# Attention scores over half the partitions: the second score matmul on the two halves of the TensorE array in turn

## The chip, the cores and the metric

The kernel runs on one core of one Trainium2 chip. The metric is the device time of one execution in microseconds (us); lower is better. The kernel before took 701.67 us, the median of three runs between 701.51 and 701.72.

## What is computed

The reference is one decoder layer in float32 for 512 tokens of width 1024: a pooling mixer and a sparse attention side by side, merged by gates, then a gated MLP with a short convolution. The change touches the attention scores. Cut to those:

```python
q  = partial_rope(rms_norm(q, q_norm_g), positions)        # 8 heads of 64, 2 groups of 4 heads
ks = partial_rope(rms_norm(k_sel, k_norm_g[1]), positions) # "selected" keys, one per group
kw = partial_rope(rms_norm(k_win, k_norm_g[2]), positions) # "window" keys, one per group
s  = jnp.einsum('bqgrd,bkgd->bgrqk', qc, kwc) * scale      # and the same with the selected keys
p  = masked_softmax(s, m_win, -1)
o  = jnp.einsum('bgrqk,bkgd->bqgrd', p, vwc)
```

With 512 tokens every block is selected and the window holds every earlier token, so both branches are causal attention, each with its own keys and values.

## The kernel before, in words

**Products in two parts.** Each operand is kept as a high and a low part, both in the type fp32r, and a product is the sum of matmuls over those parts. For the scores a head has only 64 dimensions, so the kernel stacks the parts of q on the 128 partitions: `qk_transpose` (L706 to L721) turns `qs` (per token the high 64 values beside the low 64) into `QT[g, t]`, with the high part of q on partitions 0 to 63 and the low part on 64 to 127, for four heads of group g and the 128 tokens of tile t. The keys are stored twice over: `KT[0, t]` holds the high part of k on both halves, `KT[1, t]` the low part on both halves. One matmul over all 128 partitions with `KT[0]` then gives high times high plus low times high; a second with `KT[1]` gives high times low plus low times low.

**Scores.** `scores(h, i)` (L940) computes head h for the 128 queries of tile i against the n = i + 1 key tiles up to it: for each key tile j two matmuls (s = 0 and 1) with 128x128 weights from `QT` and 256 moving columns (128 window keys and 128 selected keys) from `KT`, all in one unit that is not broken up on TensorE. Key tiles 0 and 1 fall in one PSUM bank and 2 and 3 in another. Units with n above 2 use the tag `sc` (one buffer), the others the tag `tr`. One head has four units with n from 1 to 4, 20 matmuls; eight heads have 32 units and 160 matmuls. After it come the softmax on VectorE and ScalarE (tiles `pp`, `asm`), the transposes of the probabilities (`transposes`, L975), the product with the values (`av`, L987) and `av_out` (L1011). The loop at L1034 goes through the heads; while head h is transposed and multiplied with the values, the scores of head h + 1 are computed, for i = 3, 2, 1, 0 in steps 0, 3, 6 and 10 of the head. So the units with the `QT` of group 0 end in head 2, and the last of group 1 in head 6.

**Two streams on TensorE.** The attention belongs to a stream "m". Beside it runs a stream "f" (L746 to L827): 22 "features", each 24 matmuls of 128x128 weights by 512 columns (`feature`, L733), whose results go through a pooling chain (`pool_in`, L759, pages `u`, `ps`, `pm`, `pmh`, `pml`), a small product (`mix`, L785, pages `yph` and `ypl`, kept until the last `pool_out`), or a gate (`gate`, L777, page `th`, written to DRAM and freed). In order: two features for the compressed keys, `pool_in(0)`, then three times `pool_in`, `gate`, `mix`, then a last `gate` and `mix`, then the rest of the gates with four `pool_out`.

**The planner.** No order is written out. Every call is recorded (`Plan.note`, L157) with a price (`Plan.price`, L197; for a matmul by its moving columns alone), and `Plan.run` (L226) makes an order for all engines: on TensorE each stream keeps its own order and the planner picks between the two heads of the streams; on the other engines it takes the ready operation that is due first. `Plan.emit` (L374) tries 12 orders. On the chip, each engine then runs its list strictly in that order.

**Pages.** Most tiles are "pages" of 128 partitions by 512 words, drawn from one pool of 54 (`PAGES`, L51). A page is held from its first writer to its last reader. The rule at L288 lets an operation of stream f take a page only while more than `RESERVE` = 3 pages (L61) are free, so stream f can fill the pool up to 51 and no further; stream m may use all 54.

While the attention runs, stream m and the inputs hold 16 pages of the normalised input (`xh`, `xl`, needed by every feature), 4 of values (`vv`), 8 of `QT`, 8 of `KT`, 4 zero-padded probability tiles (`PZ`, L969) and 1 or 2 of compressed scores (`cs`); later 2 pages of attention output (`oh`, `ol`) are added after each second head.

Of the kernel before, what the change touches and what calls it, by code (L numbers as in the profile page):

```python
# [9 lines left out]
F32R = mybir.dt.float32r  # L10
# [5 lines left out]
P = 128  # L16
# [380 lines left out]
def hybrid_layer(ctx: ExitStack, tc: tile.TileContext, xT, pos, par, cst, poolw, w1, wa, wb, wf,  # L397
# [3 lines left out]
    PE, ACT, DVE, POOL, SP = pl.engines  # L401
# [5 lines left out]
    def f32(ap):  # L407
        return ap.bitcast(F32)

    def page(name, shape=(P, T), dt=F32):  # L410
        return pl.tile(sb, shape, dt, name, "pg", PAGES)
# [6 lines left out]
    def keep(name, shape, dt=F32, bufs=1):  # L418
        return pl.tile(sb, shape, dt, name, "t_" + name, bufs)

    def bank(tag, shape=(P, T)):
        return pl.tile(ps, shape, F32, tag, tag, {"mm": 2, "tr": 3, "av": 1, "sc": 1}[tag], psum=True)

    def split(dst_hi, dst_lo, src, scale=None):
        if scale is None:
            ACT.activation(dst_hi, src, AF.Copy)
            DVE.tensor_sub(dst_lo, src, f32(dst_hi))
        else:
            ACT.activation(dst_hi, src, AF.Copy, scale=scale)
            DVE.scalar_tensor_tensor(dst_lo, src, scale, f32(dst_hi), op0=ALU.mult, op1=ALU.subtract)  # L430
# [62 lines left out]
    pt = bank("mm")  # L493
# [153 lines left out]
    for t in range(NT):  # L647
        pt = bank("mm")
# [21 lines left out]
    def rope_on(x, tmp, idx, n):  # L670
        np_ = x.shape[0]
        ct = rope[:np_, 0, idx].rearrange("p a b -> p (a b)")
        for o, i in ((0, 1), (1, 0)):
            DVE.tensor_mul(tmp[:, :, o * 8:(o + 1) * 8], x[:, :, i * 8:(i + 1) * 8],
                           rope[:np_, 1, idx, o][:, None, :].to_broadcast([np_, n, 8]))
        DVE.tensor_mul(x[:, :, 0:16], x[:, :, 0:16], ct[:, None, :].to_broadcast([np_, n, 16]))
        DVE.tensor_add(x[:, :, 0:16], x[:, :, 0:16], tmp)
# [3 lines left out]
    def rope_split(t):  # L681
        x, y = qp[t], kp[t]
        DVE.tensor_mul(x[:, :, 0:16], x[:, :, 0:16], gq[:, None, :].to_broadcast([P, 8, 16]))
        y4 = y.rearrange("p (b g) d -> p b g d", b=2)
        DVE.tensor_mul(y4, y4, gkv[:, 1:3][:, :, None, :].to_broadcast([P, 2, 2, DH]))
        tmp = page("rt", (P, 12, 16))
        rope_on(x, tmp[:, 0:8], t, 8)
        rope_on(y, tmp[:, 8:12], t, 4)
        qs = [page("qs", (P, 4, 2, DH), F32R) for _ in range(2)]
        ks = [page("ks", (P, 4, 2, DH), F32R) for _ in range(2)]  # L690
        for g in range(2):
            split(qs[g][:, :, 0], qs[g][:, :, 1], x[:, 4 * g:4 * g + 4])
        kx = y[:, :, None, :].to_broadcast([P, 4, 2, DH])
        split(ks[0], ks[1], kx)
        qsp.append(qs)
        ksp.append(ks)

    for t in range(NT):
        x, y = qp[t], kp[t]
# [1 line left out]
        DVE.tensor_mul(y, pskt[:, t // 2, t % 2].rearrange("p (h d) -> p h d", d=DH),  # L701
                       rs_t[:, t, 8:12][:, :, None].to_broadcast([P, 4, DH]))
    pl.span = [pl.last().i, 0]
    QT, KT = {}, {}

    def qk_transpose(t):  # L706
        for g in range(2):
            pt = bank("tr", (P, 4, P))
            with pl.unit():
                for i in range(4):  # L710
                    PE.transpose(pt[:, i], f32(qsp[t][g][:, i].rearrange("p a d -> p (a d)")), ident)
            QT[g, t] = page("qt", (P, 4, P), F32R)
            ACT.activation(QT[g, t], pt, AF.Copy)
        for s in range(2):
            pt = bank("tr", (P, 2, 2, P))
            with pl.unit():
                for g in range(2):
                    for b in range(2):
                        PE.transpose(pt[:, g, b], f32(ksp[t][s][:, 2 * b + g].rearrange("p a d -> p (a d)")), ident)
            KT[s, t] = page("kt", (P, 2, 2, P), F32R)  # L720
            ACT.activation(KT[s, t], pt, AF.Copy)  # L721

    rope_split(0)
    rope_split(1)
    turned = []
    for t in range(NT):
        qk_transpose(t)
        turned.append(pl.last())
        if t + 2 < NT:
            with pl.behind(turned[t]):  # L730
                rope_split(t + 2)

    def feature(i, hi, lo):  # L733
        wh, wl = weights(flat(wf[i]), 1024)
        pt = bank("mm")
        mm3(pt, wh, wl, hi, lo, 0, KD)
        return pt
# [8 lines left out]
    with pl.on("f"):  # L746
        for i in range(2):
            pt = feature(i, xh, xl)
# [81 lines left out]
    for i in range(2):  # L830
# [4 lines left out]
        pt = bank("tr")  # L835
# [20 lines left out]
    x = keep("kcx", (64, 1, DH))  # L856
# [83 lines left out]
    def scores(h, i):  # L940
        g, hh = divmod(h, 4)
        n = i + 1
        pt = bank("sc", (P, 4, 2, P)) if n > 2 else bank("tr", (P, 2, 2, P))
        with pl.unit():
            for j in range(n):
                for s in range(2):
                    PE.matmul(pt[:, j], QT[g, i][:, hh], KT[s, j][:, g], start=(s == 0 and j % 2 == 0),
                              stop=(s == 1), skip_group_check=True)
        sm = keep("asm", (P, 4, 2), bufs=4)
        if n > 2:  # L950
            pp = [pl.tile(sb, (P, T), F32, "pp", "pp", 10)[:, :n * P].rearrange("p (j k) -> p j k", k=P) for _ in range(2)]
        else:
            x = pl.tile(sb, (P, T), F32, "pp", "pp", 10).rearrange("p (b j k) -> p b j k", b=2, k=P)
            pp = [x[:, b, :n] for b in range(2)]
        for b in range(2):
            DVE.tensor_tensor_reduce(out=pp[b], in0=pt[:, 0:n, b], in1=mask[:, NT - n:NT], scale=1.0,
                                     scalar=3.0e38, op0=ALU.add, op1=ALU.min, accum_out=sm[:, 0, b:b + 1])
        for b in range(2):
            ACT.activation(pp[b], pp[b], AF.Exp, bias=sm[:, 0, b:b + 1], scale=-1.0,
                           accum_out=sm[:, 1, b:b + 1])  # L960
        DVE.reciprocal(sm[:, 2], sm[:, 1])
        DVE.tensor_mul(sm[:, 3], sm[:, 2], gates[:, i, 3 * h + 1:3 * h + 3])
        for b in range(2):
            DVE.tensor_scalar_mul(pp[b], pp[b], sm[:, 3, b:b + 1])
            Pt[h, b, i] = pp[b]
# [56 lines left out]

    compress_kt()
    scores(0, 0)
    cmp_scores(0)
    cmp_scores(1)
    scores(0, 1)
    cmp_softmax(0)
    scores(0, 2)
    scores(0, 3)  # L1030
    extra = {(0, 2 * i + 2): (lambda i=i: cmp_transpose(0, i)) for i in range(NT)}
# [20 lines left out]
    def any_bank():  # L1052
        turn[0] += 1
        return bank(("mm", "tr", "tr", "mm", "tr", "av")[turn[0] % 6])

    mh, ml, nots = [], [], []
    for c in range(4):
        wh, wl = weights(wno[c].rearrange("p a k n -> p (a k n)"), 1024, "v")
        for f in (2 * c, 2 * c + 1):
            o = (f % 2) * 512  # L1060
            pt = any_bank()
# [21 lines left out]
    for f in (0, 4, 1, 5, 2, 6, 3, 7):  # L1083
# [4 lines left out]
        pt = any_bank()  # L1088
# [228 lines left out]
    for f in range(8):  # L1317
        wh, wl = weights(flat(wdz[f]), 768, "v")
        pt = any_bank()
# [6 lines left out]
        for h in range(2):  # L1326
            s = slice(h * H2, (h + 1) * H2)
            pt = any_bank() if h else pt
            for k in range(16, KF):
                c = slice((k - 16) * P, (k - 15) * P)  # L1330
                with pl.unit():
                    for j, (w, q) in enumerate(((wh, yh), (wh, yl), (wl, yh))):
                        PE.matmul(back(pt[:, :H2]), w[:, c], back(q[k][:, s]), start=k == 16 and j == 0,
                                  stop=k == KF - 1 and j == 2)
# [97 lines left out]
```

## Time and profile before

| | us |
|---|---|
| median of three runs | 701.67 |
| the profiled execution | 701.34 |
| its span | 699.6 |
| TensorE matmuls busy | 693.0 |
| TensorE weight loads busy | 612.9 |
| VectorE busy | 479.1 |
| ScalarE busy | 434.4 |
| GpSimd busy | 102.9 |

The profile is of one execution. The span runs from the first to the last instruction; the execution's own time is 1.7 us more. PE is the matrix part of TensorE and PEld its weight loads; a matmul's end in the trace is modelled and matmuls overlap in the pipeline, so the time from one start to the next is what a matmul costs when the engine is full, not its duration. DVE is VectorE, ACT ScalarE, POOL GpSimd, SP the engine that only issues DMAs. Nearly every instruction has line 393, the place where the planner's order is sent out, so groups are told apart by their tiles: `sc<-kt,qt` is a score matmul with a result in the tag `sc`. A shape as 64*128 behind MATMUL or LDWEIGHTS gives the active rows and columns of the array.

### The profile page before, as it was taken

How to read it: one execution, taken by the hardware profiler on the slowest of the kernel's cores; microseconds unless marked ns; L12 is line 12 of the kernel's file. 1: busy time of each engine (PE TensorE's matmuls, PEld its weight loads, DVE VectorE, ACT ScalarE, POOL GpSimd, SP SyncE). 2: the span in 40 equal slices, each digit the busy share in tenths (PEclk: the TensorE clock that was granted, in tenths of full speed). 3: DMA queues.
4: the chain of work that ended last, by engine and by line, in shares of the span. 5: the costliest groups of instructions: out<-in, count | busy, mean ns of one | idle time of the engine just before them, and what ended most of it. 6: DMA issues, size and time to landing. Idle time of an engine off the chain costs nothing.

```text
span 699.6 us, 11376 instructions
## 1 busy us (share of the span) xinstructions
PE 693.0 (99%) x4160; PEld 612.9 (88%) x4160; DVE 479.1 (68%) x1025; ACT 434.4 (62%) x794; POOL 102.9 (15%) x127
## 2 busy tenths in 40 slices
PE   9999999999999999999999999999999999999998
PEld 8898888888888888888888898999999999999987
DVE  6868488777866653685559876777777776766542
ACT  7667378766776663443358866776777766674320
POOL 0011300010011010000012222321312212220000
PEclk9999999999999999999999999999999999999999
DMA  8576352555565657854468878897988877865131
GB/s 296 171 181 203 85 121 77 135 138 120 135 166 144 157 125 212 297 164 138 151 145 207 186 177 172 205 202 181 216 191 196 198 167 178 179 144 123 45 125 64
DMA packets 45704, 114.01 MB, mean 163 GB/s; under 512 B 5328, under 2 KB 6096, under 8 KB 45648
## 3 DMA queue, kind: packets, MB, share of 16 engines
q1 hardware_dynamic: 29664, 76.57, 33.8%
q0 software_dynamic: 15840, 36.71, 29.2%
q8 instruction: 33, 0.54, 0.3%
q14 instruction: 23, 0.19, 0.1%
q10 hardware_dynamic: 144, 0.01, 0.0%
HBM read 70.27 MB, written 6.29 MB: 109 GB/s over the span
## 4 chain that ended last, share of the span: by engine, by line
PE 96%; DMA 2%; issue 1%; DVE 1%; ACT 0%; POOL 0%; SPq 0%; POOLq 0%; DVEq 0%; ACTq 0%
PE mm L393 41%; PE tr L393 30%; PE sc L393 13%; PE av L393 11%; DMA sl<-r 1%; DMA xr<-xT 1%; POOL sl L393 0%; DVE th L393 0%; DVE kc L393 0%; ACT kt L393 0%; SPq L393 0%; DVE ks L393 0%; ACT qs L393 0%; ACT ks L393 0%; ACT xh L393 0%
## 5 line engine op out<-in xcount | busy, mean ns | idle before, releaser
L393 ACT ACTIVATE whi<-wraw 128x1024 fp32r<-128x1024 f32 (+2 forms) x97 | 98.0, 1011 | 70.0 <-issue 27.2
L393 DVE TENSOR_TENSOR wlo<-wraw,whi 128x1024 fp32r<-128x1024 f32 (+1 forms) x66 | 76.3, 1158 | 15.1 <-ACT whi L393 13.3
L393 POOL DMA_DIRECT2D wlo<-wraw x30 | 26.0, 868 | 329.9 <-ACT wlo L393 257.7
L393 PE MATMUL mm<-xh,whi 128*128 128x512 f32 x176 | 73.5, 417 | 0.9 <-DVE kc L393 0.6
L393 PE MATMUL mm<-xh,wlo 128*128 128x512 f32 x176 | 69.0, 392 | 0.0
L393 PE MATMUL mm<-xl,whi 128*128 128x512 f32 x176 | 69.0, 392 | 0.0
L393 PE MATMUL mm<-tl,sh 128*128 128x256 f32 x190 | 53.5, 282 | 0.0
L393 PE MATMUL mm<-th,sl 128*128 128x256 f32 x174 | 49.1, 282 | 0.0
L393 PE MATMUL mm<-th,sh 128*128 128x256 f32 x174 | 49.0, 281 | 0.0
L393 POOL DMA_DIRECT2D sl<-r x36 | 31.0, 862 | 89.8 <-ACT sl L393 53.4
L393 ACT ACTIVATE pp<-pp,asm 128x384 f32<-128x384 f32 (+3 forms) x64 | 35.4, 556 | 11.6 <-DVE asm L393 11.4
L393 ACT ACTIVATE wlo<-wraw 128x1024 fp32r<-128x1024 f32 x30 | 31.7, 1056 | 15.3 <-PE mm L393 6.6
L393 DVE SCALAR_TENSOR_TENSOR ft<-fg,pr,ft 128x511 f32<-128x511 f32 (+1 forms) x44 | 33.0, 749 | 12.0 <-ACT ft L393 11.3
L393 PE MATMUL sc<-yh,whi 128*128 128x512 f32 x104 | 40.5, 389 | 0.0
L393 PE MATMUL sc<-yl,whi 128*128 128x512 f32 x104 | 40.5, 389 | 0.0
L393 PE MATMUL sc<-yh,wlo 128*128 128x512 f32 x104 | 40.5, 389 | 0.0
L393 PEld LDWEIGHTS mm<-xh,wlo 128*128 128x128 f32 x176 | 33.0, 188 | 7.5
L393 PEld LDWEIGHTS mm<-xh,whi 128*128 128x128 f32 x176 | 33.2, 189 | 6.2 <-DVE th L393 1.1
L393 PEld LDWEIGHTS mm<-xl,whi 128*128 128x128 f32 x176 | 33.3, 189 | 3.6
L393 PEld LDWEIGHTS mm<-tl,sh 128*128 128x128 f32 x190 | 35.7, 188 | 0.4
L393 PEld LDWEIGHTS mm<-th,sh 128*128 128x128 f32 x174 | 32.8, 188 | 1.0
L393 PEld LDWEIGHTS mm<-th,sl 128*128 128x128 f32 x174 | 32.7, 188 | 0.0
(397 smaller groups left out, 2101.2 us busy)
## 6 DMA issues: line engine op xcount, KB each, us to landing
wlo<-wraw POOLq DMA_DIRECT2D x30, 512.0 KB, 4.6
wraw<-wup SPq DMA_DIRECT2D x26, 512.0 KB, 4.0
wraw<-wf SPq DMA_DIRECT2D x22, 512.0 KB, 3.6
r<-wup SPq DMA_DIRECT2D x36, 256.0 KB, 5.4
sl<-r POOLq DMA_DIRECT2D x36, 256.0 KB, 5.2
wraw<-wdn SPq DMA_DIRECT2D x16, 512.0 KB, 4.3
sl<-s POOLq DMA_DIRECT2D x18, 256.0 KB, 5.3
sl<-wraw POOLq DMA_DIRECT2D x18, 256.0 KB, 4.6
```

The lines of the kernel that those rows point to most:

```text
L393: getattr(self.real[o.eng], method)(*a, **kw)
```

## The change

The second score matmul leaves out low times low: it multiplies only the high part of q with the low part of k, over the 64 partitions that hold that part. For key tiles 0 and 1 (first PSUM bank) it uses partitions 0 to 63, for key tiles 2 and 3 (second bank) partitions 64 to 127, and with more than two key tiles the order is 0, 2, 1, 3, so that halves and banks alternate. The first matmuls of all key tiles now come first and the second ones after them. The number of matmuls, their moving columns and their 128 weight columns stay as they were.

For this the high part of q must lie on both halves. Group 1 now has it on the upper half from the start (the split writes high to place g and low to place 1 - g), and a new page `Q2[t]` per token tile gets, by two DMAs on GpSimd's queue, the high part of group 0 on the upper half and that of group 1 on the lower half. These are 8 DMAs of 64 partitions by 512 words (128 KB each) and 4 pages, held from the transposes to the last scores of head 7. `PAGES`, `RESERVE` and the planner's prices are unchanged.

```diff
         for g in range(2):
-            split(qs[g][:, :, 0], qs[g][:, :, 1], x[:, 4 * g:4 * g + 4])
+            split(qs[g][:, :, g], qs[g][:, :, 1 - g], x[:, 4 * g:4 * g + 4])
...
-    QT, KT = {}, {}
+    QT, KT, Q2 = {}, {}, {}
...
             QT[g, t] = page("qt", (P, 4, P), F32R)
             ACT.activation(QT[g, t], pt, AF.Copy)
+        Q2[t] = page("q2", (P, 4, P), F32R)
+        POOL.dma_start(Q2[t][64:128], QT[0, t][0:64])
+        POOL.dma_start(Q2[t][0:64], QT[1, t][64:128])
...
             for j in range(n):
-                for s in range(2):
-                    PE.matmul(pt[:, j], QT[g, i][:, hh], KT[s, j][:, g], start=(s == 0 and j % 2 == 0),
-                              stop=(s == 1), skip_group_check=True)
+                PE.matmul(pt[:, j], QT[g, i][:, hh], KT[0, j][:, g], start=(j % 2 == 0), stop=False,
+                          skip_group_check=True)
+            for j in ((0, 2, 1, 3) if n > 2 else (0, 1)):
+                if j < n:
+                    a = j // 2
+                    r = slice(a * 64, (a + 1) * 64)
+                    PE.matmul(pt[:, j], (QT[g, i] if a == g else Q2[i])[r, hh], KT[1, j][r, g], start=False, stop=True,
+                              skip_group_check=True)
```

## The prediction

> **What bounds the kernel now.** First the page: the engines' busy time and the chain that ended last.
>
> ```profile
> span 699.6 us, 11376 instructions
> PE 693.0 (99%) x4160; PEld 612.9 (88%) x4160; DVE 479.1 (68%) x1025; ACT 434.4 (62%) x794; POOL 102.9 (15%) x127
> PE 96%; DMA 2%; issue 1%; DVE 1%; ACT 0%; POOL 0%; SPq 0%; POOLq 0%; DVEq 0%; ACTq 0%
> ```
>
> TensorE is the bound: it is busy 99% of the span and carries 96% of the chain. A microsecond added to or taken from its full stream is one of the kernel's, and a stretch in which it runs dry is lost. Next, the timeline and the tile view place the change: all 160 score matmuls lie between 92 and 252 us, and the scores of heads 3 and 7 begin (for i = 3) at 144 and 236. Window sums over the stretches between those marks say what covers what.
>
> ```profile
> L393 PE MATMUL sc<-kt,qt x112: 274/282/364, 97.6 to 240.7; 128*128 128x256 f32 x112
> L393 PE MATMUL tr<-kt,qt x48: 274/282/388, 92.1 to 251.8; 128*128 128x256 f32 x48
> 144.00 0.51 PE L393 MATMUL sc<-kt,qt 128*128 128x256 f32 x3
> 235.67 0.51 PE L393 MATMUL sc<-kt,qt 128*128 128x256 f32 x3
> 97.00:144.00 47.00, 46.83 (x273) 40.10 (x272) 39.51 (x128) 36.45 (x81) 4.31 (x5) 1.00 0.46 113
> 144.00:188.00 44.00, 43.91 (x243) 36.81 (x242) 35.09 (x108) 31.91 (x68) 4.31 (x5) 1.00 0.55 139
> 188.00:236.00 48.00, 48.00 (x269) 40.36 (x268) 29.42 (x91) 33.00 (x69) 5.17 (x6) 1.00 0.57 142
> ```
>
> The columns are length, then PE, PEld, DVE, ACT and POOL busy, the clock, and DMA. In all three stretches PE is full, DVE is not far behind in the first two, and the clock is 1.00. PE is full only because stream f fills what the attention (stream m) leaves.
>
> **The change part by part.**
>
> *Matmuls.* Their number stays 160. Eight of them in a row, and the next of another kind behind, give the cost of one:
>
> ```profile
> 214.39 1.11 PE L393 MATMUL sc<-kt,qt 128*128 128x256 f32 x8
> 215.35 0.40 PE L393 MATMUL mm<-xh,whi 128*128 128x512 f32 x1
> ```
>
> 0.96 us for 8 is 0.12 each. If two matmuls on different halves ran side by side, i = 3 would save two of its four second matmuls and i = 2 one of three; i = 0 and 1 stay in one half. Three per head, 24 in all, at most 24 x 0.12 = 2.9 us; at least nothing. No row of the trace shows such a pair, so both ends stay.
>
> A rule that promises the upper end: the Trainium skill, TensorE: Matmul & The Clock Gate, section "Part 3: Packing small matmuls", says that matmuls on different row groups run concurrently, starting some 4 ns apart. By it the term is the full 2.9 us. The same page, "LDWEIGHTS (loading the stationary operand)", holds that a load costs by its columns (128/1.2 = 107 ns) whatever its rows; if loads went one by one, a pair would cost two of them and the term would be about 0.01 us a matmul. No run so far decides.
>
> *Going to 64 rows and back.* The trace has one place where the array works on 64 rows: the two transposes of `kcsp`.
>
> ```profile
> 91.31 0.39 PE L393 MATMUL mm<-xl,whi 128*128 128x512 f32 x1
> 91.54 0.39 PE L393 MATMUL mm<-xh,wlo 128*128 128x512 f32 x1
> 91.86 0.34 PE L393 MATMUL tr<-cs,kcsp 64*128 64x64 f32 x2
> 92.12 0.51 PE L393 MATMUL tr<-kt,qt 128*128 128x256 f32 x2
> 92.47 0.39 PE L393 MATMUL mm<-xh,whi 128*128 128x512 f32 x1
> ```
> ```profile
> 91.86 0.20 PEld L393 LDWEIGHTS tr<-cs,kcsp 64*128 64x128 f32 x2 [0.35 <-issue]
> 92.12 0.30 PEld L393 LDWEIGHTS tr<-kt,qt 128*128 128x128 f32 x2
> ```
> ```profile
> L393 ACT ACTIVATE kcsp<-kcx x1: 289/289/289, 89.7 to 89.7; 64x128 fp32r<-64x128 f32 x1
> L393 DVE TENSOR_TENSOR kcsp<-kcx,kcsp x1: 275/275/275, 90.2 to 90.2; 64x128 fp32r<-64x128 f32 x1
> ```
>
> Matmuls of 512 columns start 0.23 apart, with the next weights loaded meanwhile. Here the load comes only at 91.86, 0.32 after the last start, although its data were there at 90.5, and the profile calls the wait "issue": it waited for nothing that is recorded. The way back shows the same: the load at 92.12 starts together with its matmul, not ahead of it. From 91.54 to 92.47 pass 0.93 us. One matmul of 512 (0.23) and two of 256 (0.24) leave 0.46 for two small transposes, which cost 0.05 to 0.11 each (the higher is the cost of one with twice the columns, below). So a visit to 64 rows costs 0.24 to 0.35 us beyond its matmuls. A score unit has larger weights to load in the open, some 0.05 more: 0.24 to 0.40, and I take 0.32, near the middle since this is the one row. Against it stands another shape, the 128*64 matmuls of `av`:
>
> ```profile
> 206.81 0.39 PE L393 MATMUL mm<-yph,wlo 128*128 128x512 f32 x1
> 207.03 0.28 PE L393 MATMUL av<-pz,vv 128*64 128x256 f32 x1
> 207.15 0.49 PE L393 MATMUL tr<-cs,pp 128*128 128x128 f32 x3
> ```
>
> They come 0.22 behind and are followed 0.12 later: no gap (and three transposes in 0.49 with 0.27 for the last give 0.11 each). So not every smaller shape stops the array; but that one halves columns, and the 64 rows of the change are what `kcsp` has. With 32 units, each once to 64 rows and back, the price is 32 x 0.32 = 10.2 us (7.7 to 12.8) wherever PE is full.
>
> The Trainium skill, TensorEngine Tiling, "Key Properties", says that a change of tiling mode drains the array. For 64 rows the trace agrees, 0.32 instead of 0.23; for 64 columns, also a mode of that page, it does not (0.22 and 0.12).
>
> *DMAs.* Eight more on GpSimd's queue. Nearest rows:
>
> ```profile
> L393 POOL DMA_DIRECT2D wlo<-wraw x4 | 3.5, 869 | 31.8 <-ACT wlo L393 24.7 <-PE tr L393 7.1
> sl<-r POOLq DMA_DIRECT2D x36, 256.0 KB, 5.2
> L393 ACT ACTIVATE qt<-tr x8: 581/596/601, 54.6 to 71.5; 128x512 fp32r<-128x512 f32 x8
> ```
>
> 0.87 us of issue each, 7 us of an engine that between 50 and 100 us issues four DMAs and idles; about 5 us to land. The last copy of `QT` starts at 71.5 and the first score at 92.1, so 20 us hide 8. Behind a waiting DMA on that queue stand the weights' `wlo` transfers of stream f; the order puts them where they fit. I count 0, at most 2 us if a feature's weights are late once.
>
> *Pages.* This is the part that I think decides. The pool and the reserve stay, and four pages more are held until head 6. By the code, stream m and the inputs hold 16 + 4 + 8 + 8 + 4 + 1 = 41 pages in the first stretch; f may fill up to 51, so it has 10 and would have 6. After head 3 they hold 40 (`QT` of group 0 gone, four of output added), and with `Q2` 44: f has 11 and would have 7. What f needs: 2 pages of pooling weights, 2 for a group that is pooled and waits for its product, 2 more for every product done (kept to the end of the stream), and 3 at work in a pooling chain.
>
> *Stretch 1* (97 to 144; heads 0 and 1). What f did here before, and how fast attention's other engine could go alone:
>
> ```profile
> L393 PE MATMUL mm<-xh,whi 128*128 128x512 f32 x38 | 15.8, 416 | 0.2 <-DVE th L393 0.2
> ```
>
> 38 triples of 512 columns are 38 x 3 x 0.23 = 26 us, with two products 27; so m had 20 of the 47. With 6 pages f can still send TensorE two gates' features, one product and one pooling feature, 3 x 24 x 0.23 + 0.7 = 17 us; then both `mm` banks hold results for which there is no page. PE has 20 + 17 = 37, and 12 units x 0.32 = 3.8 of stops: 41 us. DVE's 39.5 falls to some 36, so PE still bounds: the stretch ends earlier, f is 10 us behind, and **3.8 us** are lost.
>
> *Stretch 2* (144 to 188; heads 2 and 3). m on PE per head: 20 scores at 0.12, 20 transposes at 0.11, per branch two matmuls each of 512, 384, 256 and 256 columns (2.6 in all), one of 512: 7.4 us. Two heads and four transposes more are 15.2; f had 28.8. Now f holds 6, may have 9, and gets through two features and two products, 12.3. PE: 27.5. DVE's 35.1 loses four or five f operations, about 3 us, and at 95% busy needs 34. Lost: **6.5 us**.
>
> *Stretch 3* (188 to 236; heads 4 and 5). f now keeps 8 (2 weights, 4 outputs, 2 pooled) but 44 + 8 is over 51: it stands still until `QT`, `KT` and `Q2` fall free in head 6. PE has m's 16.5 (two heads, 16 small transposes). DVE of before, less f's:
>
> ```profile
> L393 DVE TENSOR_TENSOR th<-mm,rb 128x512 f32<-128x512 f32 x5 | 3.5, 692 | 2.4 <-PE mm L393 2.3
> L393 DVE SCALAR_TENSOR_TENSOR th<-th,mm 128x512 f32<-128x512 f32 x2 | 1.4, 683 | 1.1 <-PE mm L393 1.1
> ```
>
> 29.4 - 4.8 = 25, at 93% 27 us. Lost: **10.5 us**; the stops hide in it. What f left undone, 10 + 16.5 + 31.5 = 58 us (48 - 16.5 = 31.5 in this stretch), is then done on PE behind the attention at its full price.
>
> *Sum.* Four units ahead of 97 and four behind 236 add 8 x 0.32 = 2.6. 3.8 + 6.5 + 10.5 + 2.6 = 23.4 us on the profiled execution's 701.34 (span 699.6 and 1.7 around it): 724.7, and since the median is 0.3 above that execution, **725 us**. Side-by-side pairs would take off at most 1.5 where PE is full; I take nothing. If DVE worked without a gap, stretches 2 and 3 would lose 4 us less; at 80% they would lose 10 more; with 0.24 and 0.40 a visit the stops move by 2. That makes 718 to 738 for this case.
>
> **The rivals.**
>
> *Only the stops count.* The planner picks among 12 orders and could fit f into fewer pages (a pooling chain before its neighbour, more f before 97). For it: PE was full with f at its limit too. Against: the counts above leave no room for the eight pages of f in stretch 3. Then 7.7 to 12.8 less up to 2.9, with 0.32 some 7 to 10: 706 to 714, likeliest 710.
>
> *No stops, only pages.* If fp32r matmuls of 64 rows pass as those of `av` do, the 6.4 us of stops in the sum go: 716 to 724, likeliest 718.
>
> *Faster: halves side by side.* Neither stops nor pages bind, and the 24 pairs overlap wholly: 701.67 - 2.9 = 698.8. The point from which it decides: a visit must cost under 2.9/32 = 0.09 us, the third part of what the `kcsp` row shows, and f must lose nothing. By the Trainium skill, TensorE: Matmul & The Clock Gate, section "Part 3: Packing small matmuls", the pairs would give just this.
>
> *The change does nothing.* No stops, pages fit, and pairs run one behind the other: 701.5 to 702.
>
> **How the numbers follow.** Pages and stops 0.58; stops alone 0.25; pages alone 0.07; faster 0.06; nothing 0.04. The range takes most of the first three, 709 to 738, and leaves out the last two and the tails, some 0.2. A measurement of this kernel tells about 0.2% (1.4 us) from no change; so faster 0.06, same 0.04, slower 0.90.
>
> **What would show it.**
>
> ```profile
> L393 DVE TENSOR_TENSOR th<-mm,rb x16: 680/692/693, 106.1 to 285.4; 128x512 f32<-128x512 f32 x16
> ```
>
> *Stops:* score rows of shape 64*128, their weight loads idle before with "issue", and a visit 0.24 to 0.40 us longer than its matmuls; if the second matmuls follow at 0.12 without a gap, that step is wrong. If in a unit with four key tiles the second ones start in pairs closer than 0.12, side by side is right. *Pages:* PE busy below 90% between about 140 and 220 us, idle ahead of score and transpose rows with DVE or ACT as releaser, the features' rows `mm<-xh` thinned out there and pushed behind the attention, and the gates' `th` row above ending far later than 285.4. If PE stays at 99% busy there and the `mm<-xh` matmuls keep their places, the page step is wrong and 710 is the time. *DMAs:* `q2` rows landing before 85 us; if scores wait for them, that zero is wrong.

## The result, and the profile after

The changed kernel takes 732.95 us, the median of four runs between 731.2 and 735.68; the kernel before took 701.59 beside it (701.33 to 701.72). The ratio is 1.0451, with a 95% interval of 1.0434 to 1.0469: 31 us slower. The forecast was 725, with a range of 709 to 738.

The page of the changed kernel: span, engines, the busy tenths of PE and its clock in 40 slices of 18.2 us, and the chain that ended last.

```profile
span 729.4 us, 11394 instructions
PE 708.9 (97%) x4160; PEld 618.1 (85%) x4160; DVE 482.0 (66%) x1025; ACT 434.0 (59%) x794; POOL 107.4 (15%) x135
PE   9999999897789999999999999999999999999998
PEclk9999999999899999999999999999999999999999
PE 92%; DVE 4%; DMA 1%; ACT 1%; issue 1%; POOL 0%; ACTq 0%; POOLq 0%; DVEq 0%
```

PE now has a hole in the slices from 128 to 219 us, and the chain has DVE in it. No other engine became the bound of the whole; the hole sits in the attention. The scores of heads 3, 5 and 7 begin (i = 3) at 139.2, 174.8 and 203.5 instead of 144.0, 188.0 and 235.7. Window sums over the stretches between these marks, with the columns as in the prediction:

```profile
97.00:139.20 42.20, 40.59 (x230) 32.04 (x229) 31.71 (x107) 30.97 (x74) 3.46 (x4) 1.00 0.40 94
139.20:174.80 35.60, 30.33 (x170) 23.90 (x169) 30.04 (x96) 24.82 (x58) 1.72 (x2) 1.00 0.33 83
174.80:203.50 28.70, 22.87 (x131) 17.87 (x130) 21.86 (x77) 18.39 (x51) 0.00 (x0) 0.88 0.00 1
```

The attention goes faster, since it has TensorE to itself, and in the third stretch not one weight tile is loaded: DMA is 0.00 and POOL, which sends the low parts of the filler's weights, does nothing. The filler stream f stands still. Its matmuls by stretch, from the groups of PE (97 to 139.2, 139.2 to 174.8, and 203.5 to 316; the third stretch has none):

```profile
L393 PE MATMUL mm<-xh,whi 128*128 128x512 f32 x24 | 10.5, 438 | 0.0
L393 PE MATMUL mm<-xh,whi 128*128 128x512 f32 x16 | 6.2, 390 | 0.0
L393 PE MATMUL mm<-xh,whi 128*128 128x512 f32 x104 | 41.9, 403 | 0.1
```

Eight of these are one feature. Three features, two, none, and then thirteen from the scores of head 7 on. Where f stops shows at its last feature ahead of the hole: the last matmul of it, and the next DVE instruction that takes a result of f, into the new page `u`.

```profile
157.12 0.40 PE L393 MATMUL mm<-xh,wlo 128*128 128x512 f32 x1
202.66 0.67 DVE L393 TENSOR_TENSOR u<-mm,rb 128x512 f32<-128x512 f32 x1
```

Between them lie 45 us in which no matmul of a feature runs, though TensorE has idle time: finished results wait to be taken. That it is the page they wait for is tested below. The last gate shows what that costs at the end:

```profile
L393 DVE TENSOR_TENSOR th<-mm,rb x16: 680/691/692, 111.9 to 315.6; 128x512 f32<-128x512 f32 x16
```

315.6 against 285.4 is 30.2 us later, and the span grew by 29.8. What follows takes its old time: 729.4 - 315.6 = 413.8 us against 699.6 - 285.4 = 414.2.

The stops are there too. One unit with four key tiles in the timeline, first PE, then PEld (`q` is `Q2`):

```profile
101.38 0.40 PE L393 MATMUL mm<-xh,wlo 128*128 128x512 f32 x1
101.61 0.94 PE L393 MATMUL sc<-kt,qt 128*128 128x256 f32 x5
102.18 0.38 PE L393 MATMUL sc<-kt,q 64*128 64x256 f32 x1
102.40 0.28 PE L393 MATMUL sc<-kt,qt 64*128 64x256 f32 x1
102.40 0.28 PE L393 MATMUL sc<-kt,q 64*128 64x256 f32 x1
102.61 0.50 PE L393 MATMUL mm<-xh,whi 128*128 128x512 f32 x1
102.95 0.39 PE L393 MATMUL mm<-xl,whi 128*128 128x512 f32 x1
```
```profile
102.18 0.18 PEld L393 LDWEIGHTS sc<-kt,q 64*128 64x128 f32 x1
102.28 0.19 PEld L393 LDWEIGHTS sc<-kt,qt 64*128 64x128 f32 x1
102.28 0.19 PEld L393 LDWEIGHTS sc<-kt,q 64*128 64x128 f32 x1
102.61 0.19 PEld L393 LDWEIGHTS mm<-xh,whi 128*128 128x128 f32 x1
```

A merged row carries the shape of its first instruction: of the five in the row at 101.61 the fifth is already a 64-row matmul; its partner on the other half has the row at 102.18. Two things are to be seen. The second matmuls run in pairs: two start at 102.40, and their loads both at 102.28. And on the way in and out the load starts with its matmul instead of ahead of it (102.18 and 102.61 in both fences), as at `kcsp`. From the unit's start to the second matmul behind it pass 102.95 - 101.61 = 1.34 us; eight matmuls at 0.12 and one of 0.23 would be 1.19. So with two pairs gained this visit still costs 0.15.

### The profile page after: what moved, and what is told of

Its sections match the earlier page's. It is cut to its first block, busy times and chain, and to the rows that moved or that the text cites. A ratio compares the mean times of both kernels' runs of the same rounds, so it can differ in the third digit from the quotient of the medians.

```text
span 729.4 us, 11394 instructions
## 1 busy us (share of the span) xinstructions
PE 708.9 (97%) x4160; PEld 618.1 (85%) x4160; DVE 482.0 (66%) x1025; ACT 434.0 (59%) x794; POOL 107.4 (15%) x135
## 4 chain that ended last, share of the span: by engine, by line
PE 92%; DVE 4%; DMA 1%; ACT 1%; issue 1%; POOL 0%; ACTq 0%; POOLq 0%; DVEq 0%
PE mm L393 40%; PE tr L393 29%; PE sc L393 13%; PE av L393 11%; DVE pp L393 1%; DMA sl<-r 1%; DVE pt L393 1%; DVE pz L393 0%; ACT pt L393 0%; POOL sl L393 0%; DVE kc L393 0%; DVE pm L393 0%; ACT kt L393 0%; DVE u L393 0%; ACT ptc L393 0%
## 5 line engine op out<-in xcount | busy, mean ns | idle before, releaser
L393 ACT ACTIVATE pp<-pp,asm 128x128 f32<-128x128 f32 (+3 forms) x64 | 35.4, 556 | 10.0 <-DVE asm L393 9.6
```

Of the source, the lines that this page charges most:

```text
L393: getattr(self.real[o.eng], method)(*a, **kw)
```

## The experiments

Each ran beside the kernel before on the same chip. In the first four that took 701.67 us, in the last four 701.79.

| kernel | us | ratio, 95% interval |
|---|---|---|
| four pages and the transfers alone | 723.13 | 1.029 to 1.0321 |
| 64 rows, one half, no page | 713.37 | 1.0153 to 1.0196 |
| the change, no page more (packed) | 711.05 | 1.0123 to 1.0154 |
| the change, two pages more | 718.63 | 1.0235 to 1.0277 |
| four pages alone, `RESERVE` = 1 | 712.71 | 1.0137 to 1.0207 |
| before, `RESERVE` = 1 | 701.5 | 0.9986 to 1.0005 |
| the eight transfers alone | 701.62 | 0.9987 to 1.0006 |
| the change for four key tiles alone | 702.57 | 1.0002 to 1.0021 |

**Theory:** the pool's rule starves f, and 64-row visits stop TensorE; two costs that stand beside each other. **Rivals:** only the stops count; only the pages count; the transfers carry part of it.

### The pages alone

```diff
+        Q2[t] = page("q2", (P, 4, P), F32R)
+        POOL.dma_start(Q2[t][64:128], QT[1, t][64:128])
+        POOL.dma_start(Q2[t][0:64], QT[1, t][0:64])
...
-                    PE.matmul(pt[:, j], QT[g, i][:, hh], KT[s, j][:, g], start=(s == 0 and j % 2 == 0),
+                    PE.matmul(pt[:, j], (Q2[i] if s and g else QT[g, i])[:, hh], KT[s, j][:, g], start=(s == 0 and j % 2 == 0),
```

> The four pages and the eight DMAs alone: all score matmuls over 128 partitions; Q2 is a plain copy of group 1's q, taken by the second matmuls of heads 4 to 7. If the page pool starves the filler stream (my theory), the filler features stand still in heads 2 to 5 as in the changed kernel and some 20 to 24 us are lost: 721 to 726 us, PE busy about 85% between 140 and 205 us. If the stops for 64 rows are what costs (rival), this is 701.5 to 703 us.

723.13 us, 21.5 above before: pages cost what the theory says, without one 64-row score matmul. Its windows between the same marks (scores of heads 3, 5 and 7 at 136.7, 170.3 and 196.5):

```profile
97.00:136.70 39.70, 37.73 (x229) 31.91 (x228) 31.69 (x107) 30.71 (x74) 3.43 (x4) 1.00 0.42 101
136.70:170.30 33.60, 28.82 (x171) 23.81 (x170) 29.48 (x97) 24.56 (x58) 1.71 (x2) 1.00 0.33 88
170.30:196.50 26.20, 19.63 (x132) 17.00 (x131) 21.95 (x77) 18.47 (x51) 0.00 (x0) 0.93 0.00 1
```

The third stretch has the same empty DMA column. Against the changed kernel each stretch is 2.0 to 2.5 us shorter. PE's share is 86% in the second and 75% in the third, where "about 85%" was expected.

### The stops alone

```diff
-        Q2[t] = page("q2", (P, 4, P), F32R)
-        POOL.dma_start(Q2[t][64:128], QT[0, t][0:64])
-        POOL.dma_start(Q2[t][0:64], QT[1, t][64:128])
...
-            for j in ((0, 2, 1, 3) if n > 2 else (0, 1)):
+            for j in (range(4)):
                 if j < n:
-                    a = j // 2
-                    r = slice(a * 64, (a + 1) * 64)
-                    PE.matmul(pt[:, j], (QT[g, i] if a == g else Q2[i])[r, hh], KT[1, j][r, g], start=False, stop=True,
+                    r = slice(g * 64, (g + 1) * 64)
+                    PE.matmul(pt[:, j], QT[g, i][r, hh], KT[1, j][r, g], start=False, stop=True,
```

> The 64-row matmuls alone: no Q2, no page more; the second matmuls of a group all use the half on which its high part of q lies, so none run side by side. Theory: PE stays full and 32 visits to 64 rows at 0.38 to 0.42 us each add 12 to 13 us: 713 to 715 us. If the stops are hidden or the pages are all there is (rival): 701.5 to 704 us. If only the pages were in the trace and stops are 0.24 each: 709.

713.37 us: 11.7 above before, 0.37 a visit. PE stays full, so every stop is paid. Its page and, in the timeline, a unit with four key tiles (the row of eight holds four matmuls over 128 rows and four over 64):

```profile
PE 705.3 (99%) x4160; PEld 616.1 (87%) x4160; DVE 479.6 (67%) x1025; ACT 435.3 (61%) x794; POOL 102.7 (14%) x127
```
```profile
101.50 1.30 PE L393 MATMUL sc<-kt,qt 128*128 128x256 f32 x8
102.73 0.50 PE L393 MATMUL mm<-xh,whi 128*128 128x512 f32 x1
103.07 0.39 PE L393 MATMUL mm<-xl,whi 128*128 128x512 f32 x1
```

103.07 - 101.50 = 1.57, less the 1.19 worked out above: 0.38 for the visit. Against 1.34 with the two pairs, a pair saves (1.57 - 1.34) / 2 = 0.115 us, a whole matmul.

### The change without more pages

`Q2` for tiles 2 and 3 alone, and the low keys in two pages:

```diff
...
-            KT[s, t] = page("kt", (P, 2, 2, P), F32R)
-            ACT.activation(KT[s, t], pt, AF.Copy)
+            if s == 0 or t < 2:
+                KT[s, t] = page("kt", (P, 2, 2, P), F32R)
+            else:
+                KT[s, t] = KT[s, t - 2]
+            r = slice(0, P) if s == 0 else slice(t // 2 * 64, (t // 2 + 1) * 64)
+            ACT.activation(KT[s, t][r], pt[r], AF.Copy)
...
```

> The change with no page more than before: Q2 only for token tiles 2 and 3 (two pages), and the low part of the keys packed into two pages instead of four, since each tile's is read on one half only. The 64-row matmuls and their pairs are those of the change. Theory: the page loss is gone, the stops stay, and 24 pairs side by side take 24 x 0.117 = 2.8 us off the one-half kernel: 710 to 712 us, 2.8 us below the kernel with one half. If pairs gain nothing: as that kernel. If the stops had been hidden: below 704.

711.05 us, 9.4 above before and 2.3 below the kernel with one half (forecast 2.8). By the two intervals that difference could be anything from 0 to 5 us; that a pair gains is shown by the timelines, 1.57 against 1.34, and not by these medians. The stops with the pairs are 9.4 us, the pages alone 21.5; together 30.9, and the change measured 31.4. So nearly the whole loss is accounted for. That the sum meets so closely is partly luck, since the starved kernels also ran some time at half clock, the changed one longest (last section). This also makes a better form of the change, but no better kernel.

### Two pages more

The packed kernel with the low keys in four pages again.

> As the packed kernel, but the low keys in four pages: two pages more than before instead of none or four. Theory: a dose between 711 and 733 us; with f allowed 8 instead of 6 pages in heads 0 and 1 and 9 in heads 4 and 5, most of the stall goes: 713 to 722, I say 717. If pages do not matter: equal to the packed kernel within 1 us.

718.63 us: two pages cost 7.6 over the packed kernel, four cost 732.95 - 711.05 = 21.9. The cost grows faster than the pages.

### The rule

```diff
-RESERVE = 3
+RESERVE = 1
```

on the kernel with the pages alone, and as a control on the kernel before.

> The kernel with the pages alone (all matmuls over 128 partitions) with RESERVE = 1 instead of 3, so that stream f may fill the pool up to 53 and gets two of the four pages back. Theory: it is this rule that starves f, and the loss falls as with two pages fewer held, by about two thirds: 706 to 714 us against 723. Rival: the m stream or a chip resource suffers from the extra pages and transfers, and the rule is not what binds: 720 to 726.

> Control for it: the kernel before with RESERVE = 1. Theory: TensorE is full there, two pages more for f gain nothing: 700.5 to 703 us. If the limit already cost something before: below 700.

712.71 us, its runs lying between 712.13 and 717.8: by the medians half of the loss is gone (two thirds were expected), with the same pages, transfers and matmuls, by two pages that f may take. The control, 701.5, cannot be told from before. The rule costs time, and only with the four pages held.

### The transfers alone

```diff
+    q2d = [pl.tile(dr, (P, 4, P), F32R, "q2d", "q2d", 4) for _ in range(4)]
...
+        POOL.dma_start(q2d[t][64:128], QT[0, t][0:64])
+        POOL.dma_start(q2d[t][0:64], QT[1, t][64:128])
```

> The eight transfers alone: the kernel before, with the same eight DMAs of 64 partitions by 512 words on GpSimd's queue, written to DRAM, so that no page is held, and read by nothing. Theory: 0 to 1 us: 701 to 703. If the transfers carry part of the 21.5 us of the pages kernel (rival): above 705.

701.62 against 701.79: nothing. These transfers go to DRAM and nothing reads them, so the run shows the price of issuing and moving them. In the changed kernel itself the eight are issued between 55.6 and 79.4, each lands within 8.1 us, and no matmul is seen to wait for one. That rival is out.

### Only where two pairs can be had

```diff
+            for j in range(n if n < 4 else 0):
+                PE.matmul(pt[:, j], QT[g, i][:, hh], KT[1, j][:, g], start=False, stop=True, skip_group_check=True)
-            for j in ((0, 2, 1, 3) if n > 2 else (0, 1)):
+            for j in ((0, 2, 1, 3) if n > 3 else ()):
```

with `Q2` for tile 3 alone.

> The change for units with four key tiles alone (i = 3): 8 visits instead of 32, 16 pairs instead of 24, Q2 for one token tile (one page more than before). Theory: 8 x (0.38 - 2 x 0.115) = 1.2 us for the visits and 0 to 3 for the page: 703 to 706. If a visit's price grew with its matmuls so that pairs pay: below 701.

702.57 us, 0.8 above before (0.1 to 1.5 by the interval) and a little under the 703 to 706 expected: the visits are 8 x 0.15 = 1.2 by the timeline. Here the page cost nothing that shows. Even the units with the most pairs do not gain.

## Why the prediction was right, point by point

*Direction and the two causes.* Both steps held: the `kcsp` row gave the stop, the count of pages gave the stall, and each alone makes the kernel slower.

*What f gets through.* Forecast 24, 16 and 0 matmuls with `whi` of `xh` (three features, two, none); measured 24, 16 and 0. Of the small products it counted one, two and none; one, one and none came. The lengths of the stretches were forecast at 41, 34 and 27 us and came out at 42.2, 35.6 and 28.7.

*The price of a visit.* Taken as 0.32 from bounds of 0.24 and 0.40; it is 0.38, and the pairs, counted at nothing, are worth 0.115 each. With both, 32 x 0.38 - 24 x 0.115 = 9.4, which is what the packed kernel measures (8.9 with the 11.7 that the kernel with one half measures for 32 visits). That the trace's one row was read at its middle and not at the end with larger loads is a small error.

*The step that failed: "the stops hide in it".* The forecast held that where f stands still the attention is bound by DVE at 93 to 95% busy, so stops on an idle PE cost nothing, and counted 6.4 us of them. In the second stretch they cost something: from the pages kernel to the changed one it grew from 33.6 to 35.6, both at a clock of 1.00, where the packed kernel's average of 9.4 / 32 = 0.29 for 8 visits is 2.3. In the third, for which the forecast said it, the growth from 26.2 to 28.7 is not all theirs: up to the scores at 193.21 in the changed kernel and at 188.05 in the other (both rows in the last section) it is 18.4 against 17.75 us at full clock, 0.7 for five visits; the other 1.9 holds three visits and a longer time at half clock. DVE was not the bound there: 21.95 of 26.2 is 84%, and 21.86 of 28.7 is 76%. The chain of the changed kernel over the third stretch, by line, says what was:

```profile
by line: PE tr L393 23.9%; PE av L393 18.7%; DVE pp L393 17.9%; PE sc L393 12.7%; DVE pt L393 6.0%; ACT pt L393 3.9%; DVE pz L393 3.6%; issue 3.2%; DVE ps L393 2.7%; DVE oraw L393 2.4%; DVE u L393 2.0%; ACT pz L393 1.7%; ACT ptc L393 1.7%; 
```

PE's transposes, products and scores are 55% of it. The attention alone is a chain that goes back and forth between PE, DVE and ACT; PE is idle a fifth of the time and still holds over half of the path. That this stretch came out near its forecast length is luck, since two errors met: DVE's work was put too high (25 against 21.9) and its share too high (93% against 76%).

*The pages' term.* Forecast at 17 us of the 23.4 (and 718 for pages alone), measured 21.5. The missing part is not in one place: the pages kernel loses in the first stretch too, 39.7 us where the forecast counted 37 of PE work, and its 3.4 us at half clock, which the forecast did not have, are worth at most half of that, 1.7 (an estimate).

*The rivals.* "Only the stops" was put at 710 and a kernel with just that is at 711.05, so its price was right and its claim, that the planner would find room, wrong. "Faster" needed a visit under 0.09 us; it is 0.38. That the pairs would run side by side, the one thing this rival had right, is shown: the rows at 102.40. The Trainium skill, TensorE: Matmul & The Clock Gate, "Part 3: Packing small matmuls", is borne out in that; the serial reading that the prediction gave beside its section "LDWEIGHTS (loading the stationary operand)" is not, since two loads start together at 102.28.

*What stays open.* The forecast took the clock as 1.00 throughout. In the profiled execution of the changed kernel it stood at 0.50 for 6.8 + 3.4 = 10.2 us, in that of the pages kernel for 3.4. Half clock costs at most half of its time, so of the 8.8 us between the two spans (729.4 and 720.6) up to 3.4 can be clock (an estimate), and the stops of the starved kernel cost 5.4 to 8.8 us. That range holds the forecast's 6.4; how far the stops hid over the whole kernel is therefore not settled. The second stretch alone, at full clock in both, shows that they did not hide there.

## What to carry to other kernels

Smaller row tiles pay only if a visit holds enough pairs: here a visit costs 0.38 us and a pair gives 0.115, so it would take four pairs (an estimate; no kernel here has them), and a unit had two at most. Before a change that holds buffers longer, count who is kept out of the pool: four pages of 54 cost 21.5 us because one stream's limit stood at 51 and the other stream held 45. And do not cost a stop at nothing because its engine idles: ask whether the work behind the stop is on the chain.

## What the runs showed of the hardware

A stretch in which PE waits can bring its clock down. In the changed kernel, by windows (third last column: the clock) and in the timeline:

```profile
192.50:193.00 0.50, 0.00 (x0) 0.00 (x0) 0.50 (x3) 0.45 (x1) 0.00 (x0) 0.89 0.00 0
193.00:199.50 6.50, 6.29 (x22) 5.02 (x23) 3.52 (x13) 3.35 (x10) 0.00 (x0) 0.50 0.00 0
199.50:200.00 0.50, 0.50 (x6) 0.50 (x5) 0.00 (x0) 0.00 (x0) 0.00 (x0) 0.79 0.18 33
207.00:209.50 2.50, 2.50 (x6) 2.04 (x7) 2.33 (x7) 0.69 (x1) 0.00 (x0) 0.50 0.28 105
```
```profile
166.50 0.59 PE L393 MATMUL sc<-kt,qt 128*128 128x256 f32 x3 [1.78 <-DVE asm L393]
188.56 0.38 PE L393 MATMUL sc<-kt,q 64*128 64x256 f32 x1
193.21 0.98 PE L393 MATMUL sc<-kt,qt 128*128 128x256 f32 x3 [3.24 <-DVE asm L393]
194.12 0.58 PE L393 MATMUL sc<-kt,q 64*128 64x256 f32 x1
206.15 0.50 PE L393 MATMUL mm<-pmh,pwh 128*128 128x512 f32 x1 [1.58 <-ACT pmh L393]
```

And in the pages kernel:

```profile
189.00:192.00 3.00, 3.00 (x14) 2.70 (x13) 2.54 (x7) 2.06 (x5) 0.00 (x0) 0.50 0.00 0
```
```profile
188.05 0.35 PE L393 MATMUL sc<-kt,qt 128*128 128x256 f32 x1 [3.24 <-DVE asm L393]
```

The clock falls from 1.00 to 0.50 some 2.9 us into the idle time of 3.24 (0.89 is the mix of the two in the window from 192.5, so the fall is at about 192.9) and is back at about 199.7, 6.8 us later; a 64-row matmul takes 0.58 us in it instead of 0.38. The same idle time of 3.24 us in the pages kernel brought half clock from about 189.0 to 192.4 (0.96 and 0.62 in the windows of half a microsecond at its ends), only 3.4 us. And in the changed kernel 3.4 us of half clock, from about 206.5 to 210 (0.54 and 0.55 at the ends), followed an idle time of 1.58 us, while 1.78 us ahead of 166.50 brought none. So the length of one wait does not decide it alone; what else does, these runs do not show. The kernel before had 1.00 throughout. The Trainium skill, TensorE: Matmul & The Clock Gate, "Part 1: The HAM clock gate", gives an idle window of some 3.4 us for the drop to half; here it came behind less, 3.24 and 1.58 us. Starving an in-order engine thus can cost twice: the idle time, and the slower work behind it.
